# Products of the next part at the head of a feed-forward, another order of its weight loads, and the last norm's factor ahead of outputs

## The chip, the cores and the metric

The kernel runs on one core of one Trainium2 chip. The metric is the device time of one execution in microseconds (us); smaller is better. Engine names: PE is TensorE, DVE is VectorE, ACT is ScalarE, POOL is GpSimd, SP is SyncE, whose in-order queue issues the DMAs.

## The reference

Two sequences, a prompt of 256 tokens and a sample of 512, go separately through a trunk of two layers of width 1024. Layer 0 mixes with a bidirectional mLSTM, layer 1 with windowed attention; after each mixer comes a feed-forward with a convolution over three tokens.

```python
def conv_ffn(h, w_up, conv_w, conv_b, w_down):
    u = h @ w_up                       # 1024 -> 2 x 2816
    u = conv over 3 tokens, per channel, + conv_b
    g = u[..., :D_FF]
    val = u[..., D_FF:]
    return (jax.nn.silu(g) * val) @ w_down

for l in range(2):
    mod = silu(c) @ adaln_w[l] + adaln_b[l]
    sh1, sc1, g1, sh2, sc2, g2 = split(mod, 6)
    x = x + g1 * mixer(rmsnorm(x, norm_g[l, 0]) * (1 + sc1) + sh1)
    h = rmsnorm(x, norm_g[l, 1]) * (1 + sc2) + sh2
    x = x + g2 * conv_ffn(h, ...)
return rmsnorm(x, final_g)
```

## The kernel before

All tokens stand side by side as 768 columns, the channels on the 128 partitions. A matrix product is made in three passes over operands split into a high and a low part (`whi`, `wlo` for weights, `zh`, `zl` and `yh`, `yl` for activations): high times high, high times low, low times high. ACT makes the high part by a cast (L222), DVE the low part by a subtraction (L223).

The feed-forward works in 11 parts. Each part has an up product for 512 of the inner channels, the convolution with silu and gate, and the down product of 256 rows, which is added to the residual (L506, `resid`). `up(p)` of one part runs beside the convolution, and `down` of the part before follows it. In the time line of layer 0 the feed-forward lies between about 533 and 1015 us, in layer 1 between about 1373 us and the end.

The up product of two weight tiles and the two halves of the columns (384 each) is made with seven products instead of eight. `pair` does this for two raw weight tiles `ra` and `rb` (128x1024 each, 512 KB): it forms sums and differences of their halves (L1052, L1054, L1055, L1078; on POOL in most parts, on DVE at the start), splits the results (`wa`, `wb`, `wc`, `s1h`/`s1l`), and calls `quarters` (L1039 to L1041) for each product with 12 matmuls of 128x384. The factors made of the activations are named `B11`, `B21` (first half of the columns alone), `T1`, `T2`, `T3`, `T4` and `B22` (the second half, or both). The order in one pair is B11, then a copy of this product to another bank (L1085), T1, T2 on top of the copy, another copy (L1092), B21, T3, B22, T4. The pieces are brought together by DVE (L1099, L1110, L1111) and ACT (L1066, L1088, L1106) in a slab (`urow`), which the convolution reads (ACT L1126, DVE L1128 and L1129, silu on ACT L1162, gate on POOL L1164).

Raw weights come by DMA through a ring of five buffers (`raw`), six loads for each part: `ra` and `rb` of two pairs and two tiles of the down product. A load can be issued when the split of the tile that had its buffer is done. The splits have three buffers each.

Part 0 stands at the head. There the norm of the second half of the columns isn't ready when the first half is, so `pair(early=True)` runs in stages: B11 and B21 of both pairs first, then T1 of both, T2, B22 and so on, each stage after DVE and ACT have made its factors (L1004 to L1028, in the generator `combined`, held by `HELD` until `advance` calls it).

Norms run as generators beside the products: `tick` counts down microseconds and calls the next step, `ready` runs a range to its end, `advance` by one step. A norm's steps: square on ACT (L102), sums on POOL (L106) and by PE, an addition on DVE (L120), the power on POOL (L123), a broadcast of the factor by PE, and the use of it. At the end of the kernel the use is `output`: eight multiplies (L498) and eight DMAs (L499) for each range of 256 columns.

The order of instructions on each engine is set by the tile framework's scheduler from the source's order and its own estimates, and each engine keeps that order.

Of the kernel before, what the change touches and what calls it, by code (L numbers as in the profile page):

```python
# [11 lines left out]
R = mybir.dt.float32r  # L12
# [3 lines left out]
P = 128  # L16
# [9 lines left out]
H = T // 2  # L26
HALVES = ((0, H, None), (H, T, None))

GAP = 4
TG = T + GAP  # L30
# [107 lines left out]
class Net:  # L138
# [357 lines left out]
    def output(self, x, pr, rng):  # L496
        for c in range(KC):
            self.nc.vector.scalar_tensor_tensor(x(c), x(c), self.cst(FG + c), pr, ALU.mult, ALU.mult)  # L498
            self.nc.sync.dma_start(self.io["y"][:, c, rng[0] : rng[1]], x(c))  # L499
        return ()  # L500


    def resid(self, xt, o, l, gc, c, rng):
# [537 lines left out]
            mm(o, wl[:, k], hi[k], start=False, stop=k == 3, skip_group_check=True)  # L1041
        self.tick(2.1)

    def pair(self, pool, u, bank, rows, early=False, spare=False, pool_adds=True):


        nc = self.nc
        r1, r2 = rows
        ra, rb = (self.load(u, h) for h in range(2))
        q = [t[:, 512 * i : 512 * (i + 1)] for t in (ra, rb) for i in range(2)]  # L1050
        tt = (nc.gpsimd if pool_adds else nc.vector).tensor_tensor
        tt(q[2], q[2], q[3], ALU.add)  # L1052
        wa = self.split(ra)
        tt(q[0], q[2], q[0], ALU.subtract)  # L1054
        tt(q[1], q[1], q[0], ALU.subtract)  # L1055
        if spare:
            s1h, s1l = (lambda t: (t[:, 0], t[:, 1]))(self.slab([P, 2, 512], R))
        else:
            s1h = pool.tile([P, 512], R, tag="s1h", name=self.nm("s1h"), bufs=1)
            s1l = pool.tile([P, 512], R, tag="s1l", name=self.nm("s1l"), bufs=1)  # L1060
        yield
        part = lambda w, i: [t[:, 512 * i : 512 * (i + 1)] for t in w]

        def evict(r, o):
            for p0, p1, _ in pieces(0, H):
                nc.scalar.copy(r[:, col(p0) : col(p0) + p1 - p0], o[:, p0:p1])  # L1066
# [11 lines left out]
        tt(q[2], q[3], q[0], ALU.subtract)  # L1078
# [12 lines left out]
        d = bank(3)  # L1091
        nc.scalar.copy(d, b)  # L1092
# [20 lines left out]
        evict(r2, d)  # L1113


    def ffn(self, l, xt, pool, apply, keep=None):
        nc = self.nc
        u0 = U_FFN + l * NPART * 3

        urow = self.slab([P, 4, TG])  # L1120
        nc.gpsimd.memset(urow[:, :, 256 : 256 + GAP], 0.0)

        def conv(u, y, ch):
            cb = self.cst(CB + l * 44 + ch)
# [5 lines left out]

        def up(p):
            pairs = []
            fixed = lambda i: self.bank[i][:, :H]
            for i in range(2):
                rows = [urow[:, 2 * i + j] for j in range(2)]
                bank = marked if p == 0 and i else fixed
                pairs.append(self.pair(pool, u0 + 3 * p + i, bank, rows, p == 0, p == 0 and i, p > 1 or p == 1 and i))
            if p == 0:
                for x in pairs:
                    next(x)  # L1140
                self.ready(HALVES[0])
                for t in self.bank[2:]:
                    mark(t[:, :H])
                for _ in range(2):
                    for x in pairs:
                        next(x)
                self.advance(HALVES[1], HELD)
                for _ in range(4):
                    for x in pairs:
                        next(x)  # L1150
                    self.advance(HALVES[1])
            for i, x in enumerate(pairs):
                for _ in x:
                    pass
                if i == 0:
                    yrow = self.slab([P, 4, TG])
                    g = self.slab([P, 2, 2, TG], R)
                for j in range(2):
                    y = yrow[:, 2 * i + j]
                    conv(urow[:, 2 * i + j], y, i * FC + 2 * p + j)  # L1160
                    if i == 0:
                        nc.scalar.activation(y, y, AF.Silu)  # L1162
                    else:
                        nc.gpsimd.tensor_tensor(y, y, yrow[:, j], ALU.mult)  # L1164
                        self.fp_copy_split(g[:, 0, j], g[:, 1, j], y)
            return g
# [230 lines left out]
```

## Time and profile before

| what | us |
|---|---|
| median of 3 runs | 1944.15 |
| lowest, highest | 1938.95, 1946.29 |
| profiled execution | 1941.91 |
| its span (first to last instruction) | 1940.1 |
| PE busy in the span | 1846.7 |
| DVE, ACT, POOL busy | 1392.0, 905.9, 506.6 |

The mean granted clock of PE is 0.981 of full speed. The span is what the page divides by; the execution's own time is 1.8 us more. A wait of an engine is shown with what ended it; idle time of an engine costs only where another waits for it in turn.

### The profile page before, as it was taken

The numbers are of one execution on the slowest core, as the hardware profiler recorded it, in microseconds if no ns is written. First come the engines' busy times: TensorE is split into PE (matmuls) and PEld (weight loads), VectorE is DVE, ScalarE is ACT, GpSimd is POOL, SyncE is SP. The second block draws the span as 40 slices with busy tenths as digits, with TensorE's granted clock in tenths as the row PEclk, the third lists the DMA queues.
The fourth block names the chain that finished last, engine by engine and source line by source line (L and its number), as shares of the span: only waits on it lengthen the run. The fifth ranks groups of instructions, "written<-read, shape, count | busy, mean of one in ns | idle before, by whom it ended". The sixth has DMA issues, their size and how long they took to land. (4 is left out here: it accounts for less than half of the span.)

```text
span 1940.1 us, 28794 instructions
## 1 busy us (share of the span) xinstructions
PE 1846.7 (95%) x11142; PEld 1672.8 (86%) x11142; DVE 1392.0 (72%) x2277; ACT 905.9 (47%) x1809; POOL 506.6 (26%) x403
## 2 busy tenths in 40 slices
PE   7898999999989999999999999999799999999997
PEld 4887887888978999999999898779799999999997
DVE  4947655774687777777777756775877777777776
ACT  3443433343455444444444555674564444444442
POOL 1011001032204333333332212332133333333323
PEclk7999999999989999999999999999899999999998
DMA  8425544545212222222222321122122222212211
GB/s 325 141 90 190 179 144 172 174 152 174 66 44 66 66 66 67 74 67 66 66 66 88 101 85 46 54 67 84 59 66 67 71 70 66 66 66 66 66 33 66
DMA packets 63380, 181.31 MB, mean 93 GB/s; under 512 B 6071, under 2 KB 23735, under 8 KB 63244
## 3 DMA queue, kind: packets, MB, share of 16 engines
q1 hardware_dynamic: 63244, 179.49, 28.5%
q8 instruction: 87, 1.43, 0.3%
q14 instruction: 49, 0.40, 0.1%
HBM read 173.03 MB, written 6.43 MB: 93 GB/s over the span
## 5 line engine op out<-in xcount | busy, mean ns | idle before, releaser
L222 ACT CAST whi<-raw 128x1024 fp32r<-128x1024 f32 x247 | 258.4, 1047 | 421.4 <-PE pa L216 203.1
L223 DVE TENSOR_TENSOR wlo<-raw,whi 128x1024 fp32r<-128x1024 f32 x247 | 331.5, 1343 | 109.1 <-ACT whi L222 108.2
L216 PE MATMUL pa<-slab,whi 128*128 128x256 f32 (+1 forms) x1472 | 348.0, 334 | 5.3 <-DVE slab L506 3.1
L216 PEld LDWEIGHTS pa<-slab,whi 128*128 128x128 f32 x1472 | 252.5, 190 | 37.2 <-DVE slab L506 9.4
L506 DVE SCALAR_TENSOR_TENSOR slab<-pa,mod,slab 128x256 f32<-128x256 f32 (+1 forms) x368 | 206.5, 591 | 58.6 <-PE pa L216 58.6
L216 PE MATMUL pa<-slab,wlo 128*128 128x256 f32 (+1 forms) x736 | 233.8, 331 | 0.0
L216 PE MATMUL ps<-zh,whi 128*128 128x256 f32 (+2 forms) x688 | 227.2, 334 | 3.4 <-ACT whi L222 1.6
L216 PE MATMUL ps<-zl,whi 128*128 128x256 f32 (+2 forms) x688 | 227.9, 333 | 0.7 <-DVE zl L477 0.7
L216 PE MATMUL ps<-zh,wlo 128*128 128x256 f32 (+2 forms) x688 | 226.9, 333 | 1.7 <-DVE wlo L223 1.7
L1039 PE MATMUL ps<-zh,whi 128*128 128x384 f32 x504 | 173.4, 344 | 19.9 <-ACT ps L1092 17.2
L1040 PE MATMUL ps<-zl,whi 128*128 128x384 f32 x504 | 170.8, 339 | 3.8 <-DVE zl L223 3.6
L1041 PE MATMUL ps<-zh,wlo 128*128 128x384 f32 x504 | 170.8, 339 | 0.0
L216 PEld LDWEIGHTS pa<-slab,wlo 128*128 128x128 f32 x736 | 139.5, 190 | 12.4
L216 PEld LDWEIGHTS ps<-zh,whi 128*128 128x128 f32 x688 | 130.6, 191 | 18.4 <-ACT whi L222 3.4
L216 PEld LDWEIGHTS ps<-zh,wlo 128*128 128x128 f32 x688 | 130.8, 190 | 12.6 <-DVE wlo L223 2.1
L216 PEld LDWEIGHTS ps<-zl,whi 128*128 128x128 f32 x688 | 130.9, 191 | 11.5 <-issue 1.7
L1052 POOL TENSOR_TENSOR raw<-raw 128x512 f32<-128x512 f32 x38 | 63.5, 1672 | 281.7 <-DMA raw<-in_w_dram 165.1
L1129 DVE SCALAR_TENSOR_TENSOR slab<-slab,cstt,slab 128x771 f32<-128x771 f32 x88 | 127.8, 1454 | 1.4
L1128 DVE SCALAR_TENSOR_TENSOR slab<-slab,cstt,slab 128x771 f32<-128x771 f32 x88 | 107.2, 1220 | 29.8 <-ACT slab L1126 29.8
L1164 POOL TENSOR_TENSOR slab<-slab 128x772 f32<-128x772 f32 x44 | 89.6, 2036 | 146.3 <-DVE slab L1129 134.7
L1039 PEld LDWEIGHTS ps<-zh,whi 128*128 128x128 f32 x504 | 95.9, 190 | 28.9 <-ACT ps L1092 23.0
L1054 POOL TENSOR_TENSOR raw<-raw,raw 128x512 f32<-128x512 f32 x38 | 49.1, 1293 | 266.5 <-DVE wlo L223 244.6
(261 smaller groups left out, 4190.2 us busy)
## 6 DMA issues: line engine op xcount, KB each, us to landing
raw<-in_w_dram SPq DMA_DIRECT2D x202, 512.0 KB, 3.7
raw<-in_adaln_w_dram SPq DMA_DIRECT2D x84, 512.0 KB, 4.3
slab<-in_x_dram SPq DMA_DIRECT2D x12, 512.0 KB, 7.0
slab<-in_adaln_w_dram SPq DMA_DIRECT2D x12, 512.0 KB, 10.2
slab<-mrows SPq DMA_DIRECT2D x8, 384.0 KB, 4.6
xs<-slab SPq DMA_DIRECT2D x6, 512.0 KB, 3.0
bt<-brow SPq DMA_DIRECT2D x16, 192.0 KB, 3.1
slab<-xs SPq DMA_DIRECT2D x6, 512.0 KB, 8.6
```

Of the source, the lines that this page charges most:

```text
L216: self.nc.tensor.matmul(out, lhsT, rhs, start=start, stop=stop)
L222: nc.scalar.copy(hi, src)
L223: nc.vector.tensor_tensor(lo, src, hi.bitcast(F32), ALU.subtract)
L506: self.nc.vector.scalar_tensor_tensor(x, o, self.mod[l][:, gc + c, q : q + 1], x, ALU.mult, ALU.add)
L1039: mm(o, wh[:, k], hi[k], start=start and k == 0, stop=False, skip_group_check=True)
L1040: mm(o, wh[:, k], lo[k], start=False, stop=False, skip_group_check=True)
L1041: mm(o, wl[:, k], hi[k], start=False, stop=k == 3, skip_group_check=True)
L1052: tt(q[2], q[2], q[3], ALU.add)
L1054: tt(q[0], q[2], q[0], ALU.subtract)
L1128: stt(y[:, 1:], u[:, :-1], w(0), y[:, 1:], ALU.mult, ALU.add)
L1129: stt(y[:, :-1], u[:, 1:], w(2), y[:, :-1], ALU.mult, ALU.add)
L1164: nc.gpsimd.tensor_tensor(y, y, yrow[:, j], ALU.mult)
```

## The change

Three edits. `pair` gets a stage ("first" for part 0, "rest" for part 1, none for the others). Line numbers in the changed file are 1 higher from `resid` on (L506 becomes L507), and 13 to 16 higher in `pair` (L1092 becomes L1103, L1052 becomes L1068).

1. In `up(0)` the first tiles `ra` of part 1's two pairs are loaded and split as well: one into a slab (`spare`), the other into the room that the factors T4 take later in `zh` and `zl`. After B11 and B21 of part 0's pairs, `outset` makes B11 and B21 of part 1's pairs, and leaves them in a second slab of rows (`urows[1]`). Part 1's pairs then take the copy of B11 from there, leave out the split of `wa`, B11 and B21, and make T1 later (`fifth`). They load both tiles again, as `wb` and `wc` need them.
2. In `pair` the second tile `rb` is loaded before `ra`.
3. `output` yields after every two channels' groups, and before the last ranges are finished, the last range's norm is advanced by one step.

```diff
     def output(self, x, pr, rng):
         for c in range(KC):
             self.nc.vector.scalar_tensor_tensor(x(c), x(c), self.cst(FG + c), pr, ALU.mult, ALU.mult)
             self.nc.sync.dma_start(self.io["y"][:, c, rng[0] : rng[1]], x(c))
-        return ()
+            if c % 2:
+                yield 1.3
...
+    def outset(self, o, w, r1):
+        part = lambda i: [t[:, 512 * i : 512 * (i + 1)] for t in w]
+        self.quarters(o, part(0), self.B11, True)
+        self.nc.scalar.copy(r1[:, col(H) :], o)
+        self.quarters(o, part(1), self.B21, False)
+        self.evict(r1, o)
+
-    def pair(self, pool, u, bank, rows, early=False, spare=False, pool_adds=True):
+    def pair(self, pool, u, bank, rows, stage=None, s1=None, pool_adds=True):
...
-        ra, rb = (self.load(u, h) for h in range(2))
+        early = stage == "first"
+        rb, ra = (self.load(u, h) for h in (1, 0))
...
         tt(q[2], q[2], q[3], ALU.add)
-        wa = self.split(ra)
+        if stage != "rest":
+            wa = self.split(ra)
         tt(q[0], q[2], q[0], ALU.subtract)
         tt(q[1], q[1], q[0], ALU.subtract)
...
-        a = bank(0)
-        self.quarters(a, part(wa, 0), self.B11, True)
-        fork = a
+        fork = r1[:, col(H) :]
         if early:
-            fork = self.tmp([P, H])
-            nc.scalar.copy(fork, a)
-            self.quarters(a, part(wa, 1), self.B21, False)
-            evict(r1, a)
+            self.outset(bank(0), wa, r1)
+        elif stage is None:
+            fork = a = bank(0)
+            self.quarters(a, part(wa, 0), self.B11, True)
         yield
...
         nc.scalar.copy(b, fork)
-        self.quarters(e, (s1h, s1l), self.T1, True)
         p5 = self.tmp([P, H])
-        nc.scalar.copy(p5, e)
+
+        def fifth():
+            self.quarters(e, (s1h, s1l), self.T1, True)
+            nc.scalar.copy(p5, e)
+
+        if stage != "rest":
+            fifth()
         yield
...
+        elif stage == "rest":
+            fifth()
         else:
             self.quarters(a, part(wa, 1), self.B21, False)
-            evict(r1, a)
+            self.evict(r1, a)
...
-        urow = self.slab([P, 4, TG])
-        nc.gpsimd.memset(urow[:, :, 256 : 256 + GAP], 0.0)
+        urows = [self.slab([P, 4, TG]) for _ in range(2)]
+        for urow in urows:
+            nc.gpsimd.memset(urow[:, :, 256 : 256 + GAP], 0.0)
...
+            urow = urows[0] if p == 0 else urows[1]
             fixed = lambda i: self.bank[i][:, :H]
+            if p == 0:
+                spare = self.slab([P, 3072], R)
+                flat = [z.rearrange("p j k t -> p (j k t)") for z in (self.zh, self.zl)]
+                ahead = [[spare[:, 1024 * (z + 1) : 1024 * (z + 2)] for z in range(2)], [z[:, 12 * H : 12 * H + 1024] for z in flat]]
+                for i, (hi, lo) in enumerate(ahead):
+                    self.fp_copy_split(hi, lo, self.load(u0 + 3 + i, 0))
...
                 for t in self.bank[2:]:
                     mark(t[:, :H])
-                for _ in range(2):
-                    for x in pairs:
-                        next(x)
+                for x in pairs:
+                    next(x)
+                for i, w in enumerate(ahead):
+                    self.outset(self.pa()[:, :H], w, urows[1][:, 2 * i])
+                for x in pairs:
+                    next(x)
                 self.advance(HALVES[1], HELD)
...
+        self.advance(RANGES[-1])
         for rng in RANGES:
             self.ready(rng)
```

More of the change, by code (lines that the diff above doesn't have):

```diff
@@ L1042, in quarters, with evict @@
         self.tick(2.1)
-    def pair(self, pool, u, bank, rows, early=False, spare=False, pool_adds=True):
+    def evict(self, r, o):
+        for p0, p1, _ in pieces(0, H):
+            self.nc.scalar.copy(r[:, col(p0) : col(p0) + p1 - p0], o[:, p0:p1])
+    def outset(self, o, w, r1):
[5 more added lines that the diff above has]
+    def pair(self, pool, u, bank, rows, stage=None, s1=None, pool_adds=True):
         nc = self.nc
         r1, r2 = rows
-        ra, rb = (self.load(u, h) for h in range(2))
+        early = stage == "first"
+        rb, ra = (self.load(u, h) for h in (1, 0))
         q = [t[:, 512 * i : 512 * (i + 1)] for t in (ra, rb) for i in range(2)]
@@ L1052, in pair @@
         tt(q[2], q[2], q[3], ALU.add)
-        wa = self.split(ra)
+        if stage != "rest":
+            wa = self.split(ra)
         tt(q[0], q[2], q[0], ALU.subtract)
         tt(q[1], q[1], q[0], ALU.subtract)
[L1056 to L1060, printed above, removed]
+        s1h, s1l = s1 or (pool.tile([P, 512], R, tag=t, name=self.nm(t), bufs=1) for t in ("s1h", "s1l"))
         yield
         part = lambda w, i: [t[:, 512 * i : 512 * (i + 1)] for t in w]
-        def evict(r, o):
-            for p0, p1, _ in pieces(0, H):
-                nc.scalar.copy(r[:, col(p0) : col(p0) + p1 - p0], o[:, p0:p1])
-        a = bank(0)
-        self.quarters(a, part(wa, 0), self.B11, True)
-        fork = a
+        fork = r1[:, col(H) :]
         if early:
-            fork = self.tmp([P, H])
-            nc.scalar.copy(fork, a)
-            self.quarters(a, part(wa, 1), self.B21, False)
-            evict(r1, a)
+            self.outset(bank(0), wa, r1)
+        elif stage is None:
+            fork = a = bank(0)
+            self.quarters(a, part(wa, 0), self.B11, True)
         yield
@@ L1112, in pair @@
         self.quarters(d, part(wb, 1), self.T4, False)
-        evict(r2, d)
+        self.evict(r2, d)
     def ffn(self, l, xt, pool, apply, keep=None):
@@ L1136, in up @@
                 bank = marked if p == 0 and i else fixed
-                pairs.append(self.pair(pool, u0 + 3 * p + i, bank, rows, p == 0, p == 0 and i, p > 1 or p == 1 and i))
+                s1 = [spare[:, 512 * z : 512 * (z + 1)] for z in range(2)] if p == 0 and i else None
+                pairs.append(
+                    self.pair(pool, u0 + 3 * p + i, bank, rows, {0: "first", 1: "rest"}.get(p), s1, p > 1 or p == 1 and i)
+                )
             if p == 0:
```

## The prediction

> **What bounds the kernel now.** I read the page first, then the waits of TensorE, then the timeline of TensorE around each wait, and last the other engines beside it. The page:
>
> ```profile
> span 1940.1 us, 28794 instructions
> PE 1846.7 (95%) x11142; PEld 1672.8 (86%) x11142; DVE 1392.0 (72%) x2277; ACT 905.9 (47%) x1809; POOL 506.6 (26%) x403
> ```
>
> TensorE is busy 1846.7 of 1940.1 us, and the change leaves the number of matmuls as it is. So only the 93 us in which it idles, and the stretches at a lower clock, can be won or enlarged. Its waits (engine and line, what it waited for, us in total, times, longest):
>
> ```profile
> PE ps L1039 <- ACT ps L1092: 17.6, 20, 3.2
> PE ps L1040 <- DVE zl L223: 10.1, 5, 3.2
> ```
>
> Both belong to the feed-forwards: the first is the copy of a half-done product (L1092) that T3 is accumulated on, the second the second-half factors at the head. The timeline of TensorE (start, us, engine, line; in brackets the idle time before, and its releaser):
>
> ```profile
> 551.37 0.69 PE L1040 MATMUL ps<-zl,s1h 128*128 128x384 f32 x1 [3.24 <-DVE zl L223]
> ...
> 561.47 0.45 PE L1040 MATMUL ps<-zl,whi 128*128 128x384 f32 x1 [1.77 <-DVE zl L223]
> ...
> 567.75 0.44 PE L1039 MATMUL ps<-bq,whi 128*128 128x384 f32 x1 [0.19 <-ACT ps L1092]
> ...
> 604.28 0.34 PE L1041 MATMUL ps<-yh,wlo 128*128 128x384 f32 x1
> 607.78 0.69 PE L1039 MATMUL ps<-zh,whi 128*128 128x384 f32 x1 [3.16 <-ACT ps L1092]
> ...
> 621.17 0.34 PE L1039 MATMUL ps<-zh,s1h 128*128 128x384 f32 x1
> ...
> 1446.26 0.44 PE L1039 MATMUL ps<-zh,whi 128*128 128x384 f32 x1 [2.11 <-ACT ps L1092]
> ```
>
> These are the head of layer 0 (551 to 568), the end of its part 1 (604 to 621) and the same place of layer 1 (1446). The windows (busy us and count of PE, PEld, DVE, ACT, POOL, then the granted clock):
>
> ```profile
> 535.00:540.00 5.00, 5.00 (x37) 5.00 (x36) 0.86 (x2) 1.29 (x3) 0.86 (x1) 1.00 0.34 108
> 545.00:570.00 25.00, 16.49 (x66) 14.55 (x65) 22.75 (x42) 13.24 (x28) 1.50 (x1) 0.80 0.14 42
> 549.50:556.33 6.83, 4.96 (x15) 4.96 (x16) 6.83 (x15) 2.05 (x4) 0.00 (x0) 0.50 0.52 154
> 607.53:610.94 3.41, 3.16 (x10) 3.16 (x11) 1.77 (x2) 2.34 (x5) 0.00 (x0) 0.50 0.00 0
> 1447.20:1450.62 3.42, 3.42 (x13) 3.42 (x12) 1.61 (x2) 1.64 (x4) 0.00 (x0) 0.50 0.16 20
> ```
>
> From 545 to 570 VectorE is busy 22.75 of 25 us: there VectorE, making the second-half factors, is the bound and TensorE waits. Just before, at 535 to 540, VectorE has worked 0.86 of 5 us, because it waits for the norm. After the long waits the clock stands at 0.50.
>
> **One steady part.** Parts 2 to 10 repeat. Around one stall of the first kind, with POOL, DVE, ACT and PE in this order:
>
> ```profile
> 1718.90 11.23 SPq L231 DMA_DIRECT2D raw<-in_w_dram  x3
> DMA to landing us min/median/max: 3.5/3.6/4.6
> 1721.18 1.29 POOL L1054 TENSOR_TENSOR raw<-raw,raw 128x512 f32<-128x512 f32 x1 [13.63 <-DVE wlo L223]
> 1722.55 1.30 POOL L1055 TENSOR_TENSOR raw<-raw 128x512 f32<-128x512 f32 x1
> 1723.80 2.02 POOL L1078 TENSOR_TENSOR raw<-raw,raw 128x512 f32<-128x512 f32 x1
> 1731.55 1.73 POOL L1052 TENSOR_TENSOR raw<-raw 128x512 f32<-128x512 f32 x1 [5.73 <-DMA raw<-in_w_dram]
> 1731.12 1.02 DVE L1129 SCALAR_TENSOR_TENSOR slab<-slab,cstt,slab 128x771 f32<-128x771 f32 x1
> 1733.32 0.62 ACT L222 CAST s1h<-raw 128x512 fp32r<-128x512 f32 x1 [2.93 <-POOL raw L1052]
> 1733.84 0.47 ACT L1092 COPY ps<-ps 128x384 f32<-128x384 f32 x1
> 1734.25 0.84 ACT L1162 ACTIVATE slab<-slab 128x772 f32<-128x772 f32 x1
> 1731.90 0.33 PE L1041 MATMUL ps<-zh,wlo 128*128 128x384 f32 x1
> 1733.31 0.34 PE L1041 MATMUL ps<-yh,wlo 128*128 128x384 f32 x1
> 1734.37 0.45 PE L1039 MATMUL ps<-zh,whi 128*128 128x384 f32 x1 [0.72 <-ACT ps L1092]
> ```
>
> T2's last matmul starts at 1731.90, so the copy of its product could run at 1732.3. It stands on ScalarE behind the cast of s1h, which waits for POOL's add (1731.55), which waits for a load. That is the second tile of the pair; the first tile's load was issued at 1718.90, and its split is only due in the next pair. The pitch of the matmuls is (1733.31 - 1731.90) / 8 = 0.176 us; T3 should start at 1733.49 and starts at 1734.37, so 0.88 us are lost.
>
> **Edit 1, the load order (steady parts).** In the changed order the second tile takes the early load. Issued at 1718.90 and landing 3.5 us later, it is there at 1722.4; its add is queued on POOL between L1071 and L1072 (before's L1054, L1055) of the pair ahead. Behind it wait L1072, L1084, the cast of wc and T2's weights. The walk: L1071 ends 1722.47, the add 1724.2 at 1.73, L1072 1725.5 to 1726.1, the cast of wc ends by 1727.1; T2 needs it at 1730.1, three microseconds later. The conv chain (silu included) slides by 0.4 us: L1143 (before's L1129) ends 1732.14 + 0.4. The order of the changed kernel puts silu (0.84) ahead of the copy, and only 2 instead of 8 matmuls between T2 and T3. So T2's last matmul starts 6 x 0.176 later, ends 1733.3; silu ends 1733.4; the copy ends 1733.9 and T3 starts there: 0.41 lost instead of 0.88. Gain 0.47 in each of 16 parts (the 20 waits without 607.78, 1446.26 and the two like 567.75): 7.5 us. Its bounds are 16 x 0.88 = 14 won, and below nothing if POOL is late (third rival).
>
> **Edit 2, products ahead (heads).** B11 and B21 of part 1's two pairs are 48 matmuls, 48 x 0.176 = 8.4 us at full clock, moved into the head where TensorE waits. They come free only if T2 (561.47 before) is not later. What is put in front of T2 on VectorE: two splits of whole tiles and two adds more. Prices, and two others needed below:
>
> ```profile
> 573.00 1.22 DVE L223 TENSOR_TENSOR wlo<-raw,whi 128x1024 fp32r<-128x1024 f32 x1 [0.35 <-ACT whi L222]
> 578.23 1.28 ACT L1162 ACT_TABLE_LOAD   x1 [1.28 <-DVE slab L1129]
> 589.33 4.90 POOL L1164 TENSOR_TENSOR slab<-slab 128x772 f32<-128x772 f32 x1 [5.32 <-ACT slab L1162]
> ```
>
> 2 x 1.22 and two adds of some 0.7, about 3.8 us, against 4.1 us that VectorE idles at 535 to 540. Walking the changed order down with before's durations puts the first second-half scaling at 540.4 to 541.2 (its gate is the landing of part 1's first-tile load, which now has to come early on SP's queue) and T2 at 561.2. I take 0.5 us late, with bounds of 0.3 early and 2.4 late (both splits uncovered). The ahead products fill the 3.24 us at 551.37; a wait of 3 to 4 us for T2's factors stays, from 557.4 by the walk.
>
> Past T2, part 1 has 48 matmuls less to cover the same VectorE and ScalarE work, and the walk shows new stalls: the table load (1.28) and silu stand ahead of a copy that T3's second half needs, 0.5 us; the cast of down's first input waits for POOL's multiply (2.8 to 4.9) with another copy behind it, 0.6 to 1.9 us. I take 2.0 per layer, bounds 1 and 8.4 (all given back). Against that the waits at 607.78 and 1446.26 go: they are edit 1's wait at its longest, with the load issued late, and in the new order that load goes out some 20 us sooner. That is 607.78 - 604.28 - 0.18 = 3.3 us plus half of 3.16 us at clock 0.50 (1.6) in layer 0, and 2.1 plus half of 3.42 (1.7) in layer 1.
>
> Layer 0: -8.4 - 4.9 + 2.0 + 0.5 = -10.8. Layer 1: -8.4 - 3.8 + 2.0 + 0.5 = -9.7. As a check on layer 0: T1 of part 2 starts at 621.17 now and near 610 by the walk. The extra memsets, two ACT copies per layer and four loads lie beside other work; without that cover the copies cost 0.5 us each.
>
> The clock terms rest on the rows above, where idle times of 3.16 and of 2.11 us are each followed by one stretch at 0.50. The Trainium skill ("TensorE: Matmul & The Clock Gate", Part 1) says that the half rate comes back after at least one idle window of about 3.4 us. By that rule the 2.11 us would cost no clock and the gain would be 1.7 us smaller; the row of 1447.20 speaks against it, so I keep the term.
>
> **Edit 3, the tail.**
>
> ```profile
> 1927.98 3.22 DVE L498 SCALAR_TENSOR_TENSOR slab<-slab,cstt,pa 128x256 f32<-128x256 f32 x8
> 1931.35 0.71 POOL L123 TENSOR_TENSOR nr<-nr,mhalf 128x2 f32<-128x2 f32 x1 [3.32 <-DVE nr L120]
> 1927.34 0.42 ACT L102 ACTIVATE nt<-slab 128x256 f32<-128x256 f32 x1 [0.35 <-DVE slab L506]
> 1932.11 1.22 PE L216 MATMUL pa<-kct,nr 128*128 128x128 f32 x4 [2.53 <-POOL nr L123]
> ```
>
> The last factor (POOL L123) waits for L120 on VectorE, behind eight output multiplies (3.22 us). The source now emits L120 first, but in the order of the changed kernel it still stands behind all eight. What has moved is TensorE's broadcast for those eight: it now follows the first two sums, which need the square of 1927.34 and POOL's add. So the eight start at about 1928.6 instead of 1927.98: 0.6 us later. The whole chain behind them shifts: +0.6, bounds 0 and 1; had L120 gone first, 3.2 would have been won.
>
> **Sum.** -10.8 - 9.7 - 7.5 + 0.6 = -27.4. The profiled execution took 1941.9 us, its span and 1.8 around it, and lies 2.2 below the median of 1944.15. So 1914.5 for a like execution, 1917 against the median.
>
> **Rivals.** (a) The heads come, the swap wins nothing, since silu or the late wc takes the copy's slot: 1917 + 7.5 = 1924. For it: the new order has 0.1 us between silu's end and T2's. (b) The heads are bound by VectorE and ScalarE further on too, and part 1 gives the 8.4 us back in each layer: 1917 + 2 x 6.4 (2.0 is counted) = 1930; with the 607.78 wait replaced by another of its size, 1938. For it: 22.75 of 25. Against: from 570 on the same window view leaves VectorE idle gaps, and my walk goes through. (c) Slower: POOL works in order, and L1072 of one pair now stands behind an add that waits for the DMA of the next. The load lands at 1722.4 and POOL is ready at 1722.47: no slack. With the landing 1.2 us later L1143 and silu push T3 to 1734.4, no better than before; each further microsecond costs 16. From 2.6 us late (6 us from issue to landing) it eats the heads too; at 4 us late the time is 1944 + 16 x 2.8 - 20 = 1969. Against it: the landings here are 3.5 to 4.6 us. (d) The scheduler's order undoes edits 1 and 2 as it undid 3: 1944; the order speaks against it. (e) The copy meets T2's end with no wait at all: 1917 - 6.5 - 3 = 1907.
>
> **How the numbers follow.** Forecast 0.45, (a) 0.17, (b) 0.16, (c) 0.08, (d) 0.06, (e) 0.08. A measurement of this kernel can tell about 0.5% from no change, 9.7 us. Faster takes the forecast, (a), (e) and three fifths of (b): 0.80; same, the rest of (b) and (d): 0.12; slower, (c): 0.08. The range runs from 1906 (case e, best T2) to 1938 (the end of b); it leaves out (c), (d) and little else.
>
> **What would show it.** Right: no wait near 607 and 1446, T1 of part 2 near 610; waits for the copy (now L1103) of some 0.3 us in steady parts; the s1h cast no longer waiting for POOL; a wait of 3 to 4 us for T2's factors at 557 to 561; the tail's eight multiplies not split by L120. Wrong: T2 after 563; waits of over 1 us in part 1 for L1103 or for the down input's cast; waits of T2 for the cast of wc; POOL's L1068 waiting for its DMA with L1072 behind it.

## The result, and the profile after

The changed kernel takes 1926.11 us (median of 4 runs, 1925.27 to 1929.58); the kernel before took 1942.06 us in the same series (median of 4, 1938.95 to 1946.29). The ratio is 0.992, with a 95% interval of 0.9895 to 0.9945: about 16 us are won, where 27 were forecast. The profiled execution took 1925.79 us, 16.1 us less than the one of before. The page of the changed kernel, its span and its engines' busy time, share and instructions:

```profile
span 1924.0 us, 28800 instructions
...
PE 1838.7 (96%) x11142; PEld 1670.9 (87%) x11142; DVE 1397.6 (73%) x2277; ACT 904.7 (47%) x1813; POOL 517.9 (27%) x405
```

The matmuls are the same 11142, and TensorE's busy time fell by 8.0 us all the same; a part of that is the clock, whose mean is 0.983 instead of 0.981. The other 8 us of the span are idle time. TensorE's waits in the changed kernel (what it waited for, us in total, times, longest):

```profile
PE ps L1040 <- ACT ps L1103: 14.9, 18, 1.9
...
PE ps L1041 <- DVE zl L223: 5.6, 2, 2.9
PE ps L1040 <- DVE slab L507: 5.1, 2, 2.8
PE pa L216 <- POOL nr L123: 3.5, 1, 3.5
```

The first line is the copy that T3 needs. Before, its 20 waits held the two long ones of 3.16 and 2.11 us; the other 18 made 17.6 - 5.3 = 12.3 us. Now 18 make 14.9 us. So the two long waits are gone, and the waits for the copy in the steady parts have not become shorter. The timeline of TensorE in the changed kernel, both heads:

```profile
534.20 0.44 PE L1040 MATMUL ps<-yh,whi 128*128 128x384 f32 x1 [2.79 <-DVE slab L507]
...
552.88 0.33 PE L1040 MATMUL ps<-zh,s1h 128*128 128x384 f32 x1
...
564.91 0.44 PE L1041 MATMUL ps<-zl,whi 128*128 128x384 f32 x1 [2.90 <-DVE zl L223]
...
611.33 0.34 PE L1040 MATMUL ps<-zh,s1h 128*128 128x384 f32 x1
...
1366.40 0.45 PE L1040 MATMUL ps<-yh,whi 128*128 128x384 f32 x1 [2.33 <-DVE slab L507]
...
1388.29 0.33 PE L1040 MATMUL ps<-zh,s1h 128*128 128x384 f32 x1
...
1447.10 0.34 PE L1040 MATMUL ps<-zh,s1h 128*128 128x384 f32 x1
```

The same entries in the kernel before (its 621.17 stands in the prediction):

```profile
533.80 0.45 PE L1039 MATMUL ps<-yh,whi 128*128 128x384 f32 x1 [1.25 <-DVE slab L506]
...
1373.35 0.44 PE L1039 MATMUL ps<-yh,whi 128*128 128x384 f32 x1 [1.55 <-DVE slab L506]
...
1459.76 0.34 PE L1039 MATMUL ps<-zh,s1h 128*128 128x384 f32 x1
```

The first matmul of each head is the entry of the feed-forward, 552.88 and 1388.29 are T1 of part 0, and 611.33 and 1447.10 are T1 of part 2. The differences of such starts say where the time came from. The last T1 of a layer starts at 1030.41 and 1870.13 us before, and at 1022.11 and 1854.27 us after.

| stretch | before | after | difference | forecast |
|---|---|---|---|---|
| start to layer 0's entry | 533.80 | 534.20 | +0.4 | 0 |
| entry to T1 of part 2, layer 0 | 87.37 | 77.13 | -10.2 | -10.8 |
| from there to the last T1 | 409.24 | 410.78 | +1.5 | half of -7.5 |
| last T1 to layer 1's entry | 342.94 | 344.29 | +1.4 | 0 |
| entry to T1 of part 2, layer 1 | 86.41 | 80.70 | -5.7 | -9.7 |
| from there to the last T1 | 410.37 | 407.17 | -3.2 | half of -7.5 |
| last T1 to the end | 69.97 | 69.73 | -0.2 | +0.6 |

The heads bring 15.9 us. The steady parts (part 2 to the last T1 of both layers) bring 1.7 of the 7.5 expected, and both entries begin after a longer wait than before (2.79 and 2.33 us for L507).

### The profile page after: what moved, and what is told of

Its sections match the earlier page's. It is cut to its first block, busy times and chain, and to the rows that moved or that the text cites. A ratio compares the mean times of both kernels' runs of the same rounds, so it can differ in the third digit from the quotient of the medians.

```text
span 1924.0 us, 28800 instructions
## 1 busy us (share of the span) xinstructions
PE 1838.7 (96%) x11142; PEld 1670.9 (87%) x11142; DVE 1397.6 (73%) x2277; ACT 904.7 (47%) x1813; POOL 517.9 (27%) x405
## 4 chain that ended last, share of the span: by engine, by line
PE 77%; DVE 10%; issue 6%; DMA 4%; ACT 2%; POOL 1%; SPq 0%; POOLq 0%; DVEq 0%; ACTq 0%
PE pa L216 25%; PE ps L216 19%; PE ps L1040 11%; PE ps L1041 10%; PE ps L1042 10%; DVE wlo L223 2%; PE pa L899 2%; DMA raw<-in_w_dram 1%; DMA slab<-in_adaln_w_dram 1%; DVE slab L507 1%; DMA raw<-in_adaln_w_dram 1%; DVE ada L433 1%; ACT whi L222 1%; POOL nt L106 1%; DVE slab L223 1%
## 5 line engine op out<-in xcount | busy, mean ns | idle before, releaser
L223 DVE TENSOR_TENSOR wlo<-raw,whi 128x1024 fp32r<-128x1024 f32 x243 | 333.8, 1375 | 118.0 <-ACT whi L222 116.9
L507 DVE SCALAR_TENSOR_TENSOR slab<-pa,mod,slab 128x256 f32<-128x256 f32 (+1 forms) x368 | 207.4, 592 | 70.3 <-PE pa L216 70.3
L216 PEld LDWEIGHTS ps<-zh,wlo 128*128 128x128 f32 x688 | 130.9, 190 | 12.8 <-DVE wlo L223 2.4
L1143 DVE SCALAR_TENSOR_TENSOR slab<-slab,cstt,slab 128x771 f32<-128x771 f32 x88 | 124.2, 1411 | 0.7
L1142 DVE SCALAR_TENSOR_TENSOR slab<-slab,cstt,slab 128x771 f32<-128x771 f32 x88 | 105.6, 1201 | 25.9 <-ACT slab L1140 25.9
L433 DVE SCALAR_TENSOR_TENSOR ada<-raw,silc,ada 128x1024 f32<-128x1024 f32 x84 | 108.3, 1322 | 8.8 <-DMA raw<-in_adaln_w_dram 8.8
## 6 DMA issues: line engine op xcount, KB each, us to landing
slab<-in_adaln_w_dram SPq DMA_DIRECT2D x12, 512.0 KB, 10.2
```

The source lines that it names most:

```text
L216: self.nc.tensor.matmul(out, lhsT, rhs, start=start, stop=stop)
L223: nc.vector.tensor_tensor(lo, src, hi.bitcast(F32), ALU.subtract)
L433: stt(acc[:, s], row, w, acc[:, s], ALU.mult, ALU.add)
L507: self.nc.vector.scalar_tensor_tensor(x, o, self.mod[l][:, gc + c, q : q + 1], x, ALU.mult, ALU.add)
L1142: stt(y[:, 1:], u[:, :-1], w(0), y[:, 1:], ALU.mult, ALU.add)
L1143: stt(y[:, :-1], u[:, 1:], w(2), y[:, :-1], ALU.mult, ALU.add)
```

## The experiments

All ratios below are against the kernel before, run on the same chip in the same series (medians 1942.34, 1940.94 and 1940.79 us in the three series). The changed kernel itself was timed in the series of the result, so a difference to it is one between medians of two series. Line numbers shift by a few where an edit adds lines.

### Each edit alone

**swap_only**: the kernel before with the load order alone.

```diff
-        ra, rb = (self.load(u, h) for h in range(2))
+        rb, ra = (self.load(u, h) for h in (1, 0))
```

> The kernel before with only the second tile's load put first. Theory (the gain of the change lies in the heads; in steady parts the wait for the copy only changes its cause): the long waits at 607.78 and 1446.26 of before go, 4.9 and 3.8 us with their clock, the sixteen steady waits stay within 0.2 us of 0.75 each, so 6 to 9 us below before. Rival 1 (the swap pays in every steady part): 7 us more, 14 to 16 below. Rival 2 (the long waits come from the ring of five buffers, not from the order of loads): within 2 us of before.

Measured: 1937.96 us, ratio 0.9983 (0.9968 to 0.9998). TensorE's waits for the copy in this kernel:

```profile
PE ps L1039 <- ACT ps L1092: 14.7, 16, 1.9
```

None of these waits stands near 607 or 1446 us any more, so the swap by itself takes away the long ones. But the 16 that are left take 14.7 us, 0.92 each, where the other 18 took 12.3 before, 0.68 each: at the copy the steady parts lose. What the swap wins in them stands at another place, the down product, and is shown further down. By the interval of the ratio 0.4 to 6.2 us are won in all, where my theory had 6 to 9.

**ahead_only**: the changed kernel with the old load order and the old tail, so that only the products ahead are left.

```diff
-        rb, ra = (self.load(u, h) for h in (1, 0))
+        ra, rb = (self.load(u, h) for h in range(2))
...
-            if c % 2:
-                yield 1.3
+        return ()
...
-        self.advance(RANGES[-1])
```

> The kernel before with only the products of part 1 made ahead. Theory: the stretch from the head's first matmul to T1 of part 2 gets 4 to 8 us shorter in each layer less the entry's new clock loss, steady parts as before (0.75 us waits), so 6 to 12 us below before, and swap_only and ahead_only add up to the change's 16 us. Rival (the long wait at the end of part 1 is the bound there, and without the swap it takes all that is won): within 3 us of before, so the two edits only pay together.

Measured: 1929.28 us, ratio 0.9934 (0.9919 to 0.9948): nearly the whole of the change. Waits, and T1 of part 2, in this kernel:

```profile
PE ps L1039 <- ACT ps L1102: 12.4, 17, 1.3
```

```profile
611.52 0.34 PE L1039 MATMUL ps<-zh,s1h 128*128 128x384 f32 x1
```

T1 of part 2 starts at 611.52 us, against 611.33 in the changed kernel. The stretch from the entry to there is 9.7 us shorter than before in layer 0 and 8.1 us in layer 1, and the time 13 us, more than my theory had (4 to 8, and 6 to 12). So the wait at 607.78 goes without the swap as well. Part 1's pairs no longer split `wa`; I take it that the raw buffer is free sooner and the load goes out sooner, but that link was only read from the code. The long waits were counted in my forecast as a gain of the swap; either edit takes them away, and they can be won only once. What the swap adds to this kernel (1929.28 to 1926.11 us) the intervals don't resolve.

**after_no_tail**: the changed kernel with the old tail.

```diff
-            if c % 2:
-                yield 1.3
+        return ()
...
-        self.advance(RANGES[-1])
```

> The changed kernel without the tail edit. Theory: the edit makes the last eight multiplies of the range before start 0.6 us later, so this runs 0 to 1 us faster than the changed kernel, and the wait of TensorE for POOL's power is 2.5 us instead of 3.5. Rival (the edit saves the chain): 1 to 3 us slower than the changed kernel.

Measured: 1928.27 us, ratio 0.9936 (0.9914 to 0.9959). The interval overlaps the changed kernel's, so the time alone says nothing on the third edit. The timeline of TensorE in this kernel does:

```profile
1918.24 1.22 PE L216 MATMUL pa<-kct,nr 128*128 128x128 f32 x4 [2.40 <-POOL nr L123]
```

The last broadcast waits 2.40 us for POOL here and 3.45 us in the changed kernel: the third edit costs about 1 us where it stands.

### What fills the steady parts

**s1l_pool**: the forecast's walk had missed the subtraction that makes `s1l` on VectorE, now between the convolution's two passes. Here it goes to POOL in the steady parts.

```diff
-        self.fp_copy_split(s1h, s1l, q[2])
+        if pool_adds and stage is None:
+            nc.scalar.copy(s1h, q[2])
+            nc.gpsimd.tensor_tensor(s1l, q[2], s1h.bitcast(F32), ALU.subtract)
+        else:
+            self.fp_copy_split(s1h, s1l, q[2])
```

> The changed kernel with the low part of s1 made by POOL instead of VectorE in parts 2 to 10. Theory (in steady parts the subtraction for s1l, 0.69 us, now runs between the two conv passes before silu, and silu stands ahead of the copy that T3 waits for): the wait of TensorE for L1103 falls from 0.8 to about 0.4 us in each of 16 parts, 4 to 8 us faster than the changed kernel. Rival 1 (the late cast of wc pushes silu): waits as they are, within 2 us of the changed kernel. Rival 2 (POOL's work slows VectorE's passes): 3 to 10 us slower.

Measured: 1929.84 us, ratio 0.994 (0.9921 to 0.9959), no gain over the changed kernel; TensorE's waits for the copy take 17.6 us. The timeline of one steady part (POOL, then DVE, then ACT):

```profile
1714.16 1.56 POOL L1085 TENSOR_TENSOR s1l<-raw,s1h 128x512 fp32r<-128x512 f32 x1 [3.23 <-ACT s1h L1084]
...
1713.56 1.02 DVE L1146 SCALAR_TENSOR_TENSOR slab<-slab,cstt,slab 128x771 f32<-128x771 f32 x1 [0.28 <-ACT slab L1144]
1714.61 1.93 DVE L1147 SCALAR_TENSOR_TENSOR slab<-slab,cstt,slab 128x771 f32<-128x771 f32 x1
...
1716.63 0.85 ACT L1194 ACTIVATE slab<-slab 128x772 f32<-128x772 f32 x1 [2.23 <-DVE slab L1147]
```

The subtraction is out of VectorE's queue, but the second pass beside it takes 1.93 instead of 1.01 us. From the start of the first pass to silu it takes 3.07 us, against 2.64 in the changed kernel (1715.77 to 1718.41, shown further down), so nothing is won: the second rival, in kind. The Trainium skill ("SBUF — State Buffer", Who interferes with whom) says that a VectorE instruction with two SBUF inputs contends with a GpSimd instruction that reads SBUF, and calls contention for the ports that the two share an exclusive lock. These rows agree: when L1147 starts, POOL has 1.11 us to go, and the pass takes 0.92 us longer.

**silu_late**: silu (L1190) is held back until the copy that T3 needs has been issued, in the steady parts; the second pair is taken four steps further first, so that this copy exists.

```diff
-        nc.scalar.copy(d, b)
+        self.forked = nc.scalar.copy(d, b).ins
...
-                    if i == 0:
+                    if i == 0 and p > 1 and j == 1:
+                        for _ in range(4):
+                            next(pairs[1])
+                        with self.tc.issue_after(self.forked):
+                            nc.scalar.activation(y, y, AF.Silu)
+                    elif i == 0:
```

> The changed kernel with the second silu of parts 2 to 10 held behind the copy (L1103) on ScalarE, the waits as they are; the order then has 4 matmuls between T2 and T3. Theory (in steady parts silu, late because s1l's subtraction runs on VectorE before the second conv pass, holds the copy): TensorE's waits for L1103 fall from 14.9 us to under 4, and the time is 8 to 12 us below the changed kernel. Rival 1 (the copy itself is late, by the cast of wc): waits of 0.4 to 0.8 us remain, 0 to 4 us faster. Rival 2 (silu after the copy delays the gate and the down product's cast, and a new wait appears there): within 2 us.

Measured: 1912.78 us, ratio 0.9841 (0.9809 to 0.9873). Waits for the copy:

```profile
PE ps L1040 <- ACT ps L1103: 1.5, 4, 0.9
```

From 14.9 us in 18 waits to 1.5 us in 4, that is 13.4 us less; the time lies 28 us below the kernel before, against 16 for the changed kernel. The intervals don't overlap. So silu in front of the copy, with only two matmuls between T2 and T3, was nearly the whole of the wait; silu_late has four, and the two weren't tried apart. An estimate from the part shown further down: the copy could start when T2's last matmul ends, at 1718.68, and starts behind silu at 1719.17, which is 0.49 of the 0.81 us lost; two more matmuls cover 0.35. This bears out the mechanism of the prediction's rival (a).

**silu_b21**: the same, and half of B21's matmuls are kept behind T2, so that six instead of two matmuls stand between T2 and T3 (silu_late alone has four).

```diff
-    def quarters(self, o, w, j, start):
+    def quarters(self, o, w, j, start, after=None):
...
+            with self.tc.issue_after(after) if after is not None and k > 1 else nullcontext():
...
-            self.quarters(a, part(wa, 1), self.B21, False)
+            self.quarters(a, part(wa, 1), self.B21, False, after=t2)
```

> As silu_late, and the second half of B21 is held behind T2 on TensorE, so that 6 matmuls stand between T2 and T3. Theory: nothing is left to win by more cover: within 2 us of silu_late. Rival 1 of silu_late (the copy is late by itself): this one is 3 to 6 us faster than silu_late.

Measured: 1908.5 us, ratio 0.9832 (0.9797 to 0.9867).

```profile
PE ps L1041 <- ACT ps L1105: 0.4, 2, 0.2
```

The rest of the waits goes, 1.1 us; the intervals of this and of silu_late don't tell their times apart.

**silu_late_no_swap**: silu_late with the old load order.

```diff
-        rb, ra = (self.load(u, h) for h in (1, 0))
+        ra, rb = (self.load(u, h) for h in range(2))
```

> silu_late with the first tile's load first again, as before the change. Theory (the swap does take the s1h cast's wait off ScalarE, and silu alone hid that): the cast of s1h stands ahead of the copy again and waits for its load, TensorE's waits for L1103 come back to 0.7 us in each of 16 parts, and the time is 9 to 14 us above silu_late, 1922 to 1928. Rival (the swap is worth nothing, and holding silu back is all of it): within 3 us of silu_late.

Measured: 1930.08 us, ratio 0.9947 (0.993 to 0.9964).

```profile
PE ps L1040 <- ACT ps L1103: 12.8, 18, 1.4
```

Without the swap, moving silu leaves 12.8 us of waits; with it, 1.5 us are left. So the swap does what the prediction said of it: it takes the wait for the load out of ScalarE's queue ahead of the copy. It showed no gain at the copy because silu stood in the same queue, ready to take the place. Two things held the copy, and each hid the worth of removing the other. The time lies 17.3 us above silu_late, more than the 9 to 14 expected: 11.3 us are these waits, and 6.2 us the wait at the down product (shown with the steady parts below), which also comes back without the swap.

### The heads

**p1_pool**: the additions on the weights of part 1's first pair go to POOL instead of VectorE, which is the bound at the head.

```diff
-                    self.pair(pool, u0 + 3 * p + i, bank, rows, {0: "first", 1: "rest"}.get(p), s1, p > 1 or p == 1 and i)
+                    self.pair(pool, u0 + 3 * p + i, bank, rows, {0: "first", 1: "rest"}.get(p), s1, p >= 1)
```

> The changed kernel with the adds of part 1's first pair on POOL instead of VectorE. Theory (at the head VectorE stands at an add that waits for part 1's first tile, landing at 541.5, and the second half's first scaling waits behind it until 542.5; four such adds lie before T2): the scaling starts by 541, the wait for T2's factors (2.9 and 2.7 us) falls by 2 to 3 us in each layer, 4 to 8 us faster than the changed kernel. Rival (POOL's own work there, an add of the same tile ahead of the norm's power, holds the factor instead): the scaling starts no earlier, within 2 us of the changed kernel or up to 4 slower.

Measured: 1931.08 us, ratio 0.9944 (0.9913 to 0.9974), no gain. The first scaling of the second half starts at 542.88 us, no earlier than in the changed kernel (542.49), which is the rival. The timeline of POOL, DVE and PE there:

```profile
558.57 4.30 POOL L1071 TENSOR_TENSOR raw<-raw,raw 128x512 f32<-128x512 f32 x1 [10.45 <-DMA raw<-in_w_dram]
...
561.65 1.64 DVE L1022 SCALAR_TENSOR_TENSOR bq<-slab,mod,bq 128x384 fp32r<-128x384 f32 x1
...
566.42 0.69 PE L1041 MATMUL ps<-zl,whi 128*128 128x384 f32 x1 [3.79 <-DVE zl L223]
```

Again the two engines delay one another: an addition that takes POOL 1.29 us in a quiet steady part takes 4.30, and two of VectorE's operations there, of 0.60 and 0.54 us otherwise, take 1.64 and 1.61. T2 comes at 566.42, 33.67 us behind the entry; in the changed kernel it is 30.71. In both tries, this one and s1l_pool, what POOL took over ran beside VectorE's operations on two SBUF operands, and nothing was won.

**late_ahead**: the splits of the tiles ahead are emitted behind the first step of part 0's pairs, not in front of it.

```diff
-                for i, (hi, lo) in enumerate(ahead):
-                    self.fp_copy_split(hi, lo, self.load(u0 + 3 + i, 0))
...
                 for x in pairs:
                     next(x)
+                for i, (hi, lo) in enumerate(ahead):
+                    self.fp_copy_split(hi, lo, self.load(u0 + 3 + i, 0))
```

> The changed kernel with the loads and splits of part 1's two first tiles put behind those of part 0. Theory (the splits run on VectorE before the last residual, and the longer wait at the entry of the feed-forward, 2.8 and 2.3 us, lowers the clock there): the wait at the entry falls to about 1.5 us, no stretch at clock 0.50 follows it, 2 to 6 us faster than the changed kernel. Rival (the split only moves behind the residual and then holds the factors of the second half): T1 and T2 come 1 to 2 us later, within 2 us of the changed kernel.

Measured: 1919.06 us, ratio 0.9878 (0.985 to 0.9906), 7 us below the changed kernel's median; the intervals just overlap, so the trace has to show it. TensorE at both entries and both T1 of part 0:

```profile
530.62 0.45 PE L1040 MATMUL ps<-yh,whi 128*128 128x384 f32 x1 [0.86 <-DVE slab L507]
...
547.73 0.34 PE L1040 MATMUL ps<-zh,s1h 128*128 128x384 f32 x1
...
1360.91 0.45 PE L1040 MATMUL ps<-yh,whi 128*128 128x384 f32 x1 [1.53 <-DVE slab L507]
...
1378.04 0.33 PE L1040 MATMUL ps<-zh,s1h 128*128 128x384 f32 x1
```

The windows behind these entries in late_ahead, and then in the changed kernel (busy us and count of PE, PEld, DVE, ACT, POOL, then the granted clock):

```profile
533.00:538.00 5.00, 5.00 (x36) 5.00 (x37) 2.16 (x4) 3.00 (x5) 0.86 (x1) 1.00 0.66 197
1363.00:1368.00 5.00, 5.00 (x38) 5.00 (x37) 3.13 (x6) 2.91 (x6) 0.86 (x1) 1.00 0.67 197
```

```profile
535.30:538.80 3.50, 3.50 (x18) 3.50 (x16) 2.92 (x4) 0.87 (x2) 0.00 (x0) 0.57 0.53 167
1367.57:1377.90 10.33, 10.33 (x41) 10.33 (x41) 4.53 (x8) 2.44 (x5) 1.25 (x1) 0.51 0.33 102
```

With the splits later the entry's wait is 0.86 and 1.53 us instead of 2.79 and 2.33, and the clock stays at 1.00. From entry to T1 it takes 17.11 and 17.13 us instead of 18.68 and 21.89: 6.3 us of clock, and 2.7 us of waiting. So the changed kernel paid for its early splits at the entry, in both layers.

Not all of this stays. T3 of part 3's second pair is a place behind the head that both traces have. In layer 1 it comes 159.92 us behind the entry (1520.83), for 164.24 in the changed kernel (1530.64); in layer 0 it comes 162.95 us behind it (693.57), for 160.88 (695.08). There new waits follow, of 2.25 us for a second-half factor (563.32) and of 1.69 us for another copy (595.82), so a cost of the rival's kind shows in layer 0 behind T1. The 8 us between the two profiles also hold a late load with its slow stretch, 2.9 us, that only the changed kernel has (the third rival, below). The sum of 9.0 and the 7 us measured agree only roughly, and the 2 to 6 of my theory were too few.

### Together

**combo**: silu_b21 and late_ahead in one kernel (no further edit).

> silu_b21 and late_ahead in one. Theory (the two act in different places, steady parts and the entry of the feed-forward): their gains over the changed kernel, 12 to 17 and 7 us, add up, 1900 to 1906. Rival (the entry's gain lay in clock stretches that fall anew in each program): 1906 to 1912, no better than silu_b21.

Measured: 1905.87 us, ratio 0.9827 (0.9809 to 0.9845). Against silu_b21 (0.9832) a further gain isn't resolved; the entries stand at waits of 0.83 and 1.49 us with 17.1 us to T1, as in late_ahead. So the 7 us of late_ahead don't show in full on top of silu_b21, and where the rest went wasn't followed; neither theory nor rival is excluded. At its end TensorE still waits 3.4 us for POOL's power.

**combo_tail**: combo, and four of the output multiplies are really held behind the last factor, as the third edit's source order suggests.

```diff
-        nc.vector.tensor_scalar(
+        factor = nc.vector.tensor_scalar(
...
+        net.factor = factor.ins
...
-            self.nc.vector.scalar_tensor_tensor(x(c), x(c), self.cst(FG + c), pr, ALU.mult, ALU.mult)
+            with self.tc.issue_after(self.factor) if rng == RANGES[1] and c > 3 else nullcontext():
+                self.nc.vector.scalar_tensor_tensor(x(c), x(c), self.cst(FG + c), pr, ALU.mult, ALU.mult)
...
+        self.advance(RANGES[1])
+        self.advance(RANGES[1])
         self.advance(RANGES[-1])
```

> combo with L120 of the last range held ahead of the last four of the eight multiplies on VectorE, and the broadcast for these eight issued ahead of the sums. Theory (the tail edit failed since VectorE's order left L120 behind all eight): TensorE's wait for POOL's power falls from 3.5 to 1.0 to 1.5 us, 1 to 2.5 us faster than combo in the profile, which the times may not resolve. Rival (the sums' end, not VectorE's order, sets L120): no change of the wait.

Measured: 1903.22 us, ratio 0.981 (0.9791 to 0.9829), the fastest version here: about 37 us below the kernel before and 23 below the changed one.

```profile
PE pa L217 <- POOL nr L124: 1.0, 1, 1.0
```

The wait falls by 2.4 us, and the median by 2.7; the intervals overlap, so the wait is what shows it.

## Why the prediction held, point by point

The direction and the range held; the gain was 16 us and not 27. The range, 1906 to 1938 us, was wide enough for rivals (a) and (b) as well, so that it held says little of the steps. These are:

**Layer 0's head: right in size, by errors that cancel.** T1 of part 2 was expected near 610 and came at 611.33; the stretch gained 10.2 of 10.8 us. Inside, T2's factor was to be 0.5 us late, and T2 starts at 564.91 instead of 561.47, 3.4 us late. By the prediction's own sign ("Wrong: T2 after 563") this step failed. VectorE in the changed kernel:

```profile
541.59 0.69 DVE L1071 TENSOR_TENSOR raw<-raw,raw 128x512 f32<-128x512 f32 x1 [1.21 <-DMA raw<-in_w_dram]
542.49 1.14 DVE L1005 SCALAR_TENSOR_TENSOR slab<-slab,gain,pa 128x384 f32<-128x384 f32 x2 [0.20 <-PE pa L216]
...
558.60 4.25 DVE L1015 SCALAR_TENSOR_TENSOR nt<-slab,mod,bq 128x384 f32<-128x384 f32 x4
```

The first scaling (L1005) starts at 542.49, where the walk had 540.4 to 541.2: an addition in front of it waits for a load. Its four operations L1015 take 4.25 us for 3.23 before (at 556.18), beside two additions on POOL where there was one. Together that is about 2.3 of the 2.9 us that were missed. Past T2 the stretch shrank from 59.70 to 46.42 us, 13.3 instead of the 8.4 + 4.9 - 2.0 = 11.3 expected: the new stalls of part 1, put at 2.0, appear as three waits of 0.2 us. That answers rival (b), by which part 1 would give back the whole 8.4.

**Layer 1's head: the failed term is the clock at the entry.** It gained 5.7 of 9.7. The stretch from entry to T1 of part 0 took 21.89 us there and 17.13 in late_ahead: 4.8 us, in the window in which the clock stands at 0.51 for 10.33 us. The prediction counted half-rate time behind the waits it removed, and not behind the longer wait that the early splits make on VectorE in front of L507. T2 starts 33.72 us behind the entry (1400.12), 29.74 in late_ahead (1390.65) and 27.66 before (1401.01), so it is 6.1 us late where 0.5 was forecast, and 4.0 of the 4.8 us reach it. Without these 4.0 the gain would have been 9.7, an estimate. That it would so have met the forecast is in part luck, since T2 would still be 2.1 us late. Layer 0's entry paid 1.6 us up to T1 in the same way.

**Steady parts: the failed step is the walk from the conv chain to silu.** Forecast 7.5 us, measured 1.7 by the starts, and the waits for the copy did not shrink. One steady part of the changed kernel (DVE, ACT, PE):

```profile
1715.77 1.02 DVE L1142 SCALAR_TENSOR_TENSOR slab<-slab,cstt,slab 128x771 f32<-128x771 f32 x1 [0.28 <-ACT slab L1140]
1716.71 0.68 DVE L223 TENSOR_TENSOR s1l<-raw,s1h 128x512 fp32r<-128x512 f32 x1
1717.31 1.01 DVE L1143 SCALAR_TENSOR_TENSOR slab<-slab,cstt,slab 128x771 f32<-128x771 f32 x1
...
1715.64 0.60 ACT L222 CAST s1h<-raw 128x512 fp32r<-128x512 f32 x1
...
1718.41 0.85 ACT L1190 ACTIVATE slab<-slab 128x772 f32<-128x772 f32 x1 [1.80 <-DVE slab L1143]
1719.17 0.47 ACT L1103 COPY ps<-ps 128x384 f32<-128x384 f32 x1
...
1718.35 0.33 PE L1042 MATMUL ps<-zh,wlo 128*128 128x384 f32 x1
1718.70 0.34 PE L1042 MATMUL ps<-yh,wlo 128*128 128x384 f32 x1
1719.69 0.44 PE L1040 MATMUL ps<-zh,whi 128*128 128x384 f32 x1 [0.66 <-ACT ps L1103]
```

The cast of s1h waits for nothing any more, and in this part the load is in time: these steps held. But its subtraction (L223, 0.68 us) now falls between the convolution's two passes. The walk let that chain slide by 0.4 us and left the 0.68 out. So silu ends at 1719.26 and the copy runs to 1719.64. T3 should start one matmul (0.176 us) behind the one at 1718.70, at 1718.88; it starts at 1719.69. That is 0.81 us lost, for 0.88 before and 0.41 expected. It is the mechanism of rival (a), whose time of 1924 is the nearest to the result, and silu_late bears it out.

That 1.7 us were won in the steady parts all the same is luck: they come from a wait that the prediction didn't have. The start of the down product in one steady part, before and then in the changed kernel:

```profile
1705.44 0.34 PE L1041 MATMUL ps<-zh,s1l 128*128 128x384 f32 x1
1706.02 0.73 PE L216 MATMUL pa<-slab,whi 128*128 128x512 f32 x2 [0.24 <-DVE slab L506]
```

```profile
1691.37 0.34 PE L1042 MATMUL ps<-zh,s1l 128*128 128x384 f32 x1
1691.55 0.62 PE L216 MATMUL pa<-slab,whi 128*128 128x512 f32 x2
```

In the kernel before, the first matmuls of the down product come late at one such place in each of the 16 steady parts; measured up to the third of them that is 6.1 us in both layers. ahead_only and silu_late_no_swap have the same 16 places (6.2 us), and no kernel with the swap has one. Why the swap removes them wasn't followed. Against these 6.1 us, the waits for the copy between the same T1 grew by 2.6 us, and one slow stretch cost 1.7: a gain of 1.8 us by this sum, and 1.7 by the starts.

**The tail: right in kind, too small in size.** The eight multiplies are not split, and start later. The timeline of DVE:

```profile
1911.93 3.22 DVE L498 SCALAR_TENSOR_TENSOR slab<-slab,cstt,pa 128x256 f32<-128x256 f32 x8 [1.43 <-PE pa L216]
```

Measured from the last product (1927.15 us before, 1909.69 after) they start 1.4 us later than before; 0.6 was forecast, and 1 was its upper bound. The broadcast for them (1911.13) has moved behind the first sums (1910.66), as the walk said. After_no_tail shows the same 1 us in the wait for POOL.

**The third rival: no slower kernel, but its wait is there.** The prediction saw no slack between the landing of the load and POOL's L1068, with L1072 behind it, and named a wait there as a sign of being wrong. In 10 of the 16 steady parts (2 to 9 in both layers) L1068 does wait for its load, by 0.22 to 0.83 us, and T3 then waits 0.83 to 1.87 us for the copy; in the other six T3 waits 0.62 to 0.74. The worst part (POOL, ACT, PE, then the window behind it with the clock at 0.50):

```profile
873.49 2.00 POOL L1068 TENSOR_TENSOR raw<-raw 128x512 f32<-128x512 f32 x1 [0.83 <-DMA raw<-in_w_dram]
877.50 1.05 ACT L222 CAST whi<-raw 128x1024 fp32r<-128x1024 f32 x1 [1.57 <-POOL raw L1072]
885.70 0.44 PE L1040 MATMUL ps<-zh,whi 128*128 128x384 f32 x1 [1.87 <-ACT ps L1103]
886.45:889.86 3.41, 3.41 (x13) 3.41 (x12) 1.90 (x2) 1.08 (x4) 1.00 (x1) 0.50 0.13 14
```

Its wait is 1.2 us longer than the mean of the six in time, and half of 3.41 us is 1.7 more. Seven of the ten late loads lie in layer 0, this one among them: that is most of why layer 0's steady parts grew by 1.5 us while layer 1's shrank by 3.2 (the sum above, taken by layer, gives +1.2 and -3.1). Waits of 1.87 or 1.88 us stand in swap_only, after_no_tail and p1_pool too, each behind a load that POOL waits 1.0 to 1.2 us for. In silu_late POOL's wait for the load is longer still, 0.94 us in the middle, and T3 doesn't wait.

## What to carry to other kernels

When a wait in an in-order queue is removed, look at what else stands between it and the instruction that matters: here the load's wait and silu each hid the other, and only both edits together won the 13 us. Look at all repeated parts, and not at one: a load without slack was in time in six of 16 and late in ten, and a gain stood at another product than the one that was watched. Work put in front of an idle engine delays whatever it stands ahead of, so check the entry too, and not only the stretch that it shortens. Here several microseconds of clock hung on one microsecond of waiting, and two edits that remove the same wait can't both be counted.

## What the runs showed of the hardware

**The clock behind a wait of 2 to 3 us.** From the entry of the feed-forward to T1 of part 0, TensorE has the same 105 matmuls in every kernel with the products ahead (104 in the trace of p1_pool), so the distance shows what the clock cost:

| kernel | wait at entry, us | entry to T1, us |
|---|---|---|
| late_ahead, layer 0 and 1 | 0.86, 1.53 | 17.11, 17.13 |
| combo, layer 0 and 1 | 0.83, 1.49 | 17.1, 17.1 |
| ahead_only, layer 0 and 1 | 1.94, 3.03 | 17.10, 18.68 |
| s1l_pool, layer 1 and 0 | 2.15, 2.79 | 18.69, 18.67 |
| p1_pool, layer 1 and 0 | 2.29, 2.79 | 16.93, 19.11 |
| changed kernel, layer 1 and 0 | 2.33, 2.79 | 21.89, 18.68 |
| silu_b21, layer 1 and 0 | 2.40, 2.79 | 21.86, 23.28 |

Over all runs (the kernels without products ahead have a distance of their own, 13.54 us), none of the 8 entries with a wait up to 1.55 us lost clock time; of 4 between 1.68 and 1.94 us one did; of 14 from 2.15 to 3.04 us 13 did. The loss is between 1.4 and 6.2 us, and differs between executions with the same wait (18.67 and 23.28 at 2.79 us). The prediction kept the clock term for a wait of 2.11 us against the rule of the Trainium skill ("TensorE: Matmul & The Clock Gate", Part 1), by which an idle window of about 3.4 us comes before the half rate. By that rule the 3.16 us of layer 0 would have cost no clock either, which the prediction left out. These runs speak for the term and differ from the rule: waits well under 3.4 us were followed by half-rate time, and the measurement decides. What sets the length of the slow stretch isn't settled.

**VectorE and GpSimd beside each other.** I had not expected the price: a VectorE pass of 1.01 us took 1.93, operations of 0.54 and 0.60 took 1.61 and 1.64, and a POOL addition of 1.29 took 4.30, in s1l_pool and p1_pool above.
